# ScalarE's copies of the rotated keys: eight in a row, or one by one from the rounded tile

## The chip, the core and the metric

The kernel runs on one core of a Trainium2 chip. The metric is the device time of one execution in microseconds (us). Five engines work side by side, each through its own list of instructions in a fixed order: TensorE (PE in the profile; its weight loads are shown as PEld), VectorE (DVE), ScalarE (ACT), GpSimd (POOL) and SyncE (SP), which here issues nearly all the DMA transfers. An instruction that waits for a result of another engine holds up all that stands behind it in its own list.

## The reference

Two layers of a transformer trunk work on one sequence of 512 tokens with 1024 channels, in float32. Each layer does this:

```
h = rmsnorm(x);  proj = h @ w_in            # 6 x 512 columns: sb q,k,v and df q,k,v
sb_out = stick_breaking_attention(...)      # 8 heads of 64
dq, dk = rope(df_q), rope(df_k)             # 4 heads x 2 maps of 64
p = softmax(mask(dq . dk / 8))              # per head and map
df_out = rmsnorm((p[0] - lam * p[1]) @ df_v)
x = x + concat(sb_out, df_out) @ w_o
x = x + relu(rmsnorm(x) @ w_ff1)**2 @ w_ff2 # 4096 hidden channels
```

At the end comes one more rmsnorm. The change is in the keys `dk` of the differential attention, after the rotation by `rope`.

## The kernel before, in words

**Precision.** A float32 product is made of three matmuls. Each operand is split into a rounded high part (`hi`, made by a ScalarE copy) and the rest (`lo`, a VectorE subtraction); the function `three` (lines 258 to 260) multiplies hi by hi, lo by hi and hi by lo. The weights are split in the kernel too. They arrive as 512-KB units (`raw`, three buffers, issued by SP), and `split_part` makes `whi` on ScalarE (line 118) and `wlo` on VectorE (line 119), with two buffers of each. So `whi` of a unit waits until TensorE has done with the unit before the last.

**Order.** A layer begins with the projections in the order of the tuple `ORDER`: d0, w0, d1, d2, w1, d3, s0, u0 and so on. A `d` is one head of the differential group (q and k, 24 matmuls each), a `w` is its values, an `s` a pair of stick-breaking heads, a `u` their values. The generator `dense` gives these out in steps, and between the steps the generator `attn` gives out pieces of the attention of heads that are ready. A modelled clock (`clock[0]`, in us) decides how they are mixed, and `defer` hands a function over once that clock has gone on by a given time. The order in which the instructions are handed over is a priority; a scheduler at build time then lays down the list of each engine by its own estimate of durations. So a few instructions handed over later can change the lists of all engines.

**A `d` head.** `evict_d` (line 466 and after) multiplies the q and the k block in PSUM with `cos_t` and `sin_t` on VectorE (lines 469 and 470; tiles u and v). For k it defers `rest` by 3.5 us (`DLY_R`). There POOL subtracts and adds (lines 477 and 478), which gives two tiles: `u1` (named u0d1q and so on in the profile) with the first halves of all rotated vectors, and `v1` (v0d1q) with the second halves. Each tile holds q in partitions 0 to 63 and k in 64 to 127. Each is split into hi and lo (lines 205 and 206; h0d1k and l0d1k in the profile), and then the 32-row pieces are brought into the layout that the score matmuls want, once for each tile j and map m: four DMAs (line 446), two into the q stack (st..q, of hi and lo) and two into the stack of the keys' low parts (kl..), and two ScalarE copies of 32x512 into the stack of the keys' high parts (st..k, lines 493 and 494). That makes 16 DMAs and 8 copies for a head. The copies read the float32 tile (u1 or v1) and round it on the way, so they need POOL's result alone and not the split. The scores of the head may begin 10 us (`DLY_D`) of the modelled clock after `rest`.

**Scores.** `scores` puts 128 queries against up to 512 keys into a PSUM bank S (two buffers; lines 505 and 506). VectorE masks and takes the maximum (lines 545 to 550), ScalarE does the exponentials (line 558), and these release the bank for the scores after next. The weights p are normalised by DVE and POOL (lines 564 to 567), transposed on TensorE (line 586, T), split again (zh, zl, fh, fl) and multiplied with the values (O). The hi and lo tiles of the heads and the diagonal tiles of the norms (dgh, dgl) share one pool of four buffers (`tr`).

Of the kernel before, what the change touches and what calls it, by code (L numbers as in the profile page):

```python
# [9 lines left out]
F32 = mybir.dt.float32  # L10
F32R = mybir.dt.float32r
BF16 = mybir.dt.bfloat16
AF = mybir.ActivationFunctionType
# [24 lines left out]
RA, RB = (21, 8), (26, 16)  # L38
MAN = ()
_CTX = {}  # L40
DLY_R, DLY_D, DLY_S = 3.5, 10.0, 6.0
TAIL, ATT, DENSE, CAP = 6.0, 54.0, 145.0, 0.1
SBQ, SBK, SBV, DFQ, DFK, DFV = (i * 512 for i in range(6))
# [96 lines left out]
def trunk(ctx, tc, xT, w, gains, lamv, cos, sin, out):  # L140
    nc = tc.nc
# [62 lines left out]
    def split(hi, lo, src):  # L204
        nc.scalar.activation(hi, src, AF.Copy)  # L205
        nc.vector.tensor_tensor(out=lo, in0=src, in1=hi.bitcast(F32), op=ALU.subtract)  # L206
# [142 lines left out]
    for l in range(L):  # L349
        with ExitStack() as actx:  # L350
# [18 lines left out]
            def tt(name):  # L369
                return a2.tile([P, S], F32, tag="t", name=name, bufs=4)  # L370

            def tr(name):
                return a2.tile([P, S], F32R, tag="hl", name=name, bufs=4)
# [57 lines left out]
            def defer(delay, fn):  # L431
                later.append((clock[0] + delay, fn))
                later.sort(key=lambda e: e[0])

            def stack_tiles(kind, b, which):
                nm = f"{l}{kind}{b}{which}"
                i = "ds".index(kind) * 4 + b
                assert i < 2 or scored[i - 2] == (2 if i < 6 else 4), (nm, scored)
                out = [a2.tile([P, 2, S], F32R, tag="st" + which, name="st" + nm)]
                if which == "k":  # L440
                    out.append(a2.tile([P, 2, S], F32R, tag="kl", name="kl" + nm))
                stacks[(kind, b, which)] = out
                return out

            def move(dst, src):
                nc.sync.dma_start(dst.bitcast(F32), src.bitcast(F32))

            def evict_s(pt, kind, b, which):
# [14 lines left out]
                if which == "k":  # L463
                    ready[(kind, b)] = clock[0] + DLY_S

            def evict_d(pt, kind, b, which):
                nm = f"{l}{kind}{b}{which}"
                u, v = tt("u" + nm), tt("v" + nm)
                nc.vector.tensor_mul(u, pt, cos_t)
                nc.vector.tensor_mul(v, pt, sin_t)  # L470
                if which == "q":
                    heads[("x", b)] = (u, v)
                    return
                u1, v1 = heads.pop(("x", b))

                def rest():
                    nc.gpsimd.tensor_sub(u1, u1, v)
                    nc.gpsimd.tensor_add(v1, v1, u)
                    q, = stack_tiles(kind, b, "q")
                    k, kl = stack_tiles(kind, b, "k")  # L480
                    for j, o in enumerate((u1, v1)):
                        hi, lo = tr(f"h{nm}{j}"), tr(f"l{nm}{j}")
                        split(hi, lo, o)
                        d0 = slice(32 * j, 32 * j + 32)
                        d1 = slice(64 + 32 * j, 64 + 32 * j + 32)
                        for m in range(2):
                            rq = slice(32 * m, 32 * m + 32)
                            rk = slice(64 + 32 * m, 64 + 32 * m + 32)
                            move(q[d0, m, :], hi[rq, :])
                            move(q[d1, m, :], lo[rq, :])  # L490
                            move(kl[d0, m, :], lo[rk, :])
                            move(kl[d1, m, :], lo[rk, :])
                            nc.scalar.activation(k[d0, m, :], o[rk, :], AF.Copy)
                            nc.scalar.activation(k[d1, m, :], o[rk, :], AF.Copy)
                    ready[(kind, b)] = clock[0] + DLY_D

                defer(DLY_R, rest)

            def scores(pt, st, m, i):
# [405 lines left out]
```

## Time and profile before

Three runs took 1244.31, 1244.63 and 1246.58 us (median 1244.63). The profiled execution took 1240.59 us; its span from the first to the last instruction is 1238.8 us.

| engine | busy us | share of the span | instructions |
|---|---|---|---|
| PE | 1197.8 | 97% | 5978 |
| DVE | 685.4 | 55% | 1009 |
| ACT | 553.2 | 45% | 948 |
| POOL | 207.2 | 17% | 267 |

TensorE's granted clock over the span was 0.991. The projections and attention of layer 0 lie at about 5 to 270 us, those of layer 1 at about 615 to 880 us; the rest is the MLP. The shares are averages of very unlike stages: in the MLP ScalarE is busy for two to four tenths of the time, and in the stretches with the `d` heads for five to seven tenths. A row of a timeline gives the start, the duration, the engine, the line, the operation with output and inputs, and in brackets how long the engine was idle before and what ended that.

### The profile page before, as it was taken

What the parts mean: (1) busy time and instruction counts of PE and PEld (TensorE: products, weight loads), DVE (VectorE), ACT (ScalarE), POOL (GpSimd) and SP (SyncE); (2) the same over time, 40 slices, a digit from 0 to 9 for tenths busy, and PEclk for the clock granted to TensorE, in tenths of its full rate; (3) what the DMA queues carried; (4) which work ended last, traced back from release to release, by engine and by line L of the source; (5) the groups of instructions that cost most, each with busy time, mean ns of one, the idle gap of its engine ahead of it and who ended that gap; (6) DMA issues with size and microseconds to landing.
All of it is one profiled execution on the core that took longest, in us unless ns stands there. A gap on an engine that the chain in (4) does not pass through costs nothing. (4 is left out here: it accounts for less than half of the span.)

```text
span 1238.8 us, 15970 instructions
## 1 busy us (share of the span) xinstructions
PE 1197.8 (97%) x5978; PEld 1007.3 (81%) x5978; DVE 685.4 (55%) x1009; ACT 553.2 (45%) x948; POOL 207.2 (17%) x267
## 2 busy tenths in 40 slices
PE   7899999999999999999999999999999999999996
PEld 5787898888888888888887888888888888888886
DVE  6676779875443234433346867787644223444325
ACT  5665656654332224433346656665444212433214
POOL 4123354330000000001112225432200000000002
PEclk9999999999999999999999999999999999999998
DMA  6343435223322332332333354342333332322231
GB/s 209 104 122 113 132 98 151 86 71 102 102 90 98 102 97 90 102 101 88 100 97 115 96 143 113 100 128 64 101 95 94 102 99 89 101 102 86 93 94 68
DMA packets 46892, 128.20 MB, mean 103 GB/s; under 512 B 7264, under 2 KB 10336, under 8 KB 46816
## 3 DMA queue, kind: packets, MB, share of 16 engines
q1 hardware_dynamic: 46672, 127.17, 33.8%
q8 instruction: 47, 0.77, 0.2%
q14 instruction: 29, 0.24, 0.1%
q10 hardware_dynamic: 144, 0.02, 0.0%
HBM read 104.09 MB, written 2.10 MB: 86 GB/s over the span
## 5 line engine op out<-in xcount | busy, mean ns | idle before, releaser
L118 ACT ACTIVATE whi<-raw 128x1024 fp32r<-128x1024 f32 (+2 forms) x200 | 204.9, 1026 | 490.3 <-PE f L259 427.7
L119 DVE TENSOR_TENSOR wlo<-raw,whi 128x1024 fp32r<-128x1024 f32 (+2 forms) x200 | 247.6, 1239 | 164.2 <-ACT whi L118 162.8
L258 PE MATMUL f<-h_hi,whi 128*128 128x512 f32 x512 | 199.4, 389 | 0.0
L259 PE MATMUL f<-h_lo,whi 128*128 128x512 f32 x512 | 199.2, 389 | 0.0
L260 PE MATMUL f<-h_hi,wlo 128*128 128x512 f32 x512 | 199.2, 389 | 0.0
L259 PE MATMUL f<-ul,whi 128*128 128x512 f32 x496 | 193.0, 389 | 0.0
L258 PE MATMUL f<-uh,whi 128*128 128x512 f32 x496 | 193.0, 389 | 0.0
L260 PE MATMUL f<-uh,wlo 128*128 128x512 f32 x496 | 193.0, 389 | 0.0
L805 DVE SCALAR_TENSOR_TENSOR ft<-f,rbc 128x512 f32<-128x512 f32 x64 | 44.2, 691 | 164.0 <-PE f L260 163.1
L258 PEld LDWEIGHTS f<-h_hi,whi 128*128 128x128 f32 x512 | 96.1, 188 | 20.1
L260 PEld LDWEIGHTS f<-h_hi,wlo 128*128 128x128 f32 x512 | 96.1, 188 | 19.8
L259 PEld LDWEIGHTS f<-h_lo,whi 128*128 128x128 f32 x512 | 96.1, 188 | 19.8
L258 PEld LDWEIGHTS f<-uh,whi 128*128 128x128 f32 x496 | 93.1, 188 | 19.5
L260 PEld LDWEIGHTS f<-uh,wlo 128*128 128x128 f32 x496 | 93.1, 188 | 19.3
L259 PEld LDWEIGHTS f<-ul,whi 128*128 128x128 f32 x496 | 93.1, 188 | 19.2
L223 POOL TENSOR_TENSOR ssq<-ssq,sq 128x512 f32<-128x512 f32 x28 | 41.8, 1491 | 377.4 <-ACT sq L222 368.0
L834 DVE TENSOR_TENSOR x<-x,f 128x512 f32<-128x512 f32 x32 | 22.0, 687 | 103.1 <-PE f L260 103.1
L340 POOL TENSOR_TENSOR ssq<-ssq,sqf 128x256 f32<-128x256 f32 x6 | 4.4, 736 | 338.3 <-ACT sqf L338 335.0
L206 DVE TENSOR_TENSOR ul<-fu,uh 128x512 fp32r<-128x512 f32 x64 | 44.1, 692 | 0.4 <-ACT uh L205 0.4
L205 ACT ACTIVATE uh<-fu 128x512 fp32r<-128x512 f32 x64 | 40.5, 633 | 2.0
L806 ACT ACTIVATE fu<-ft 128x512 f32<-128x512 f32 x64 | 39.6, 618 | 1.6 <-DVE ft L805 1.6
L526 POOL TENSOR_TENSOR sig1s<-sig1s,C1s 128x128 f32<-128x128 f32 (+3 forms) x32 | 29.0, 907 | 53.0 <-DVE C1s L523 38.7
(650 smaller groups left out, 2301.2 us busy)
## 6 DMA issues: line engine op xcount, KB each, us to landing
raw<-in_w SPq DMA_DIRECT2D x176, 512.0 KB, 3.6
raw<-in_w SPq DMA_DIRECT2D x16, 448.0 KB, 3.2
x<-in_xT SPq DMA_DIRECT2D x8, 256.0 KB, 4.5
out_xT<-y SPq DMA_DIRECT2D x8, 256.0 KB, 2.4
raw<-in_w SPq DMA_DIRECT2D x8, 128.0 KB, 4.5
cos_t<-in_cos SPq DMA_DIRECT2D x2, 256.0 KB, 4.0
sin_t<-in_sin SPq DMA_DIRECT2D x2, 256.0 KB, 4.3
kl0d0k<-l0d0k SPq DMA_DIRECT2D x8, 64.0 KB, 2.0
```

The source lines that it names most:

```text
L118: nc.scalar.activation(hi[:, a:b], raw[:, a:b], AF.Copy)
L119: nc.vector.tensor_tensor(out=lo[:, a:b], in0=raw[:, a:b], in1=hi[:, a:b].bitcast(F32), op=ALU.subtract)
L205: nc.scalar.activation(hi, src, AF.Copy)
L206: nc.vector.tensor_tensor(out=lo, in0=src, in1=hi.bitcast(F32), op=ALU.subtract)
L223: eng.tensor_tensor(out=ssq, in0=ssq, in1=sq, op=ALU.add)
L258: nc.tensor.matmul(pt, ah, bh, start=first, stop=False)
L259: nc.tensor.matmul(pt, ah, bl, start=False, stop=False)
L260: nc.tensor.matmul(pt, al, bh, start=False, stop=last)
L526: nc.gpsimd.tensor_mul(sig[:, 0:wd], sig[:, 0:wd], C[:, 1 : wd + 1])
L805: nc.vector.scalar_tensor_tensor(out=t, in0=pt, scalar=0.0, in1=rbc, op0=ALU.max, op1=ALU.mult)
L806: nc.scalar.activation(uu, t, AF.Square)
L834: nc.vector.tensor_add(x[:, db, :], x[:, db, :], pt)
```

## The change

The two copies of each (j, m) are no longer handed over at once with the rest of the head. Each is handed to `defer` by itself: the first 0.9 us (`KC_GAP`) of the modelled clock after `rest`, the second 1.8 us, and so on to the eighth at 7.2 us. And a copy now reads the rounded tile `hi` (h0d1k in the profile) and not the float32 tile `o` (u0d1q or v0d1q). The copied values are the same, since a rounded value does not change when it is rounded again. The number and the shape of the instructions stay as they were.

```diff
+KC_GAP = 0.9
...
+            def copy_k(dst, src):
+                return lambda: nc.scalar.activation(dst, src.bitcast(F32), AF.Copy)
...
-                            nc.scalar.activation(k[d0, m, :], o[rk, :], AF.Copy)
-                            nc.scalar.activation(k[d1, m, :], o[rk, :], AF.Copy)
+                            for i, d_ in enumerate((d0, d1)):
+                                defer(KC_GAP * (4 * j + 2 * m + i + 1), copy_k(k[d_, m, :], hi[rk, :]))
```

## The prediction, made before the result was known

> **What bounds the kernel.** I read the page first:
>
> ```profile
> span 1238.8 us, 15970 instructions
> PE 1197.8 (97%) x5978; PEld 1007.3 (81%) x5978; DVE 685.4 (55%) x1009; ACT 553.2 (45%) x948; POOL 207.2 (17%) x267
> ```
>
> TensorE bounds the whole. A change on ScalarE can only add to or take from TensorE's idle 41 us, and from the time it works at a lower clock. So the second view is what TensorE waited for (total, times, longest):
>
> ```profile
> PE S0d L505 <- ACT p0d L558: 3.9, 3, 2.7
> PE S1d L505 <- ACT p1d L558: 3.6, 2, 2.0
> PE S1d L505 <- DMA st1d3q<-l1d3k: 2.7, 1, 2.7
> ...
> PE p1d1q L258 <- ACT whi L118: 2.1, 1, 2.1
> ...
> PE T0d L586 <- DVE fl0d L206: 1.6, 1, 1.6
> PE p0u L412 <- ACT whi L118: 1.5, 1, 1.5
> ```
>
> The first and second rows, the two with `whi`, and the DMA row (its source is a split of ScalarE's) stand behind ScalarE's list, where the copies are. Third, that list in time, ahead of the 2.1-us wait:
>
> ```profile
> 635.66 0.63 ACT L493 ACTIVATE st1d0k<-v1d0q 32x512 fp32r<-32x512 f32 x1 [5.26 <-POOL v1d0q L478]
> 636.31 0.63 ACT L494 ACTIVATE st1d0k<-v1d0q 32x512 fp32r<-32x512 f32 x1
> 636.96 0.63 ACT L205 ACTIVATE h1d0k<-u1d0q 128x512 fp32r<-128x512 f32 x1
> ...
> 641.49 0.63 ACT L494 ACTIVATE st1d0k<-v1d0q 32x512 fp32r<-32x512 f32 x1
> 642.14 1.06 ACT L118 ACTIVATE whi<-raw 128x1024 fp32r<-128x1024 f32 x1
> ```
>
> All eight copies and both splits of the head stand ahead of the weight split that TensorE needs at 641.1. Ahead of the 1.5-us wait it is the same:
>
> ```profile
> 111.69 0.63 ACT L205 ACTIVATE h0d3k<-u0d3q 128x512 fp32r<-128x512 f32 x1 [2.03 <-POOL u0d3q L477]
> ...
> 115.55 0.63 ACT L494 ACTIVATE st0d3k<-v0d3q 32x512 fp32r<-32x512 f32 x1
> 116.20 1.06 ACT L118 ACTIVATE whi<-raw 128x1024 fp32r<-128x1024 f32 x1
> ```
>
> Last, the clock by 1-us windows (length, PE, PEld, DVE, ACT and POOL busy, granted clock, DMA):
>
> ```profile
> 643.00:644.00 1.00, 0.73 (x2) 0.30 (x2) 0.78 (x1) 1.00 (x4) 0.00 (x0) 1.00 0.31 78
> 644.00:645.00 1.00, 0.50 (x1) 0.50 (x2) 1.00 (x3) 0.99 (x2) 0.00 (x0) 0.51 0.49 123
> 645.00:646.00 1.00, 1.00 (x4) 0.71 (x4) 1.00 (x2) 0.74 (x2) 0.00 (x0) 0.50 0.37 94
> ```
>
> After a long wait the clock is halved for some 3.4 us (here 644.0 to 647.4), which costs 1.7 us of TensorE's time. In the stages with attention this comes four times: after waits of 2.66 us (to 81.3), 1.50 and 0.87 us together (to 118.6), 2.14 us (to 643.3) and 2.68 us (to 728.9). It does not come after 1.90 us (33.6) or 2.05 us (685.2). So I charge 1.7 us for a wait above about 2.4 us.
>
> [...]
>
> **What the change moves.** No instruction is added. The 64 copies stay at 0.628 us (lines 493 and 494), 40.2 us of ScalarE. Sixteen of them now wait for a split on their own engine. The dependent pair fu, uh in the MLP has 0.04 us between them (302.94 + 0.61 to 303.59) against 0.01 between independent copies; the largest gap that the trace puts down to ScalarE itself is 0.38 us (before `whi` at 45.68). That is 0.5 to 6 us in all; I take 0.5, as the pair has the same shape, and it lies beside TensorE's work. The lists that the changed kernel's build lays down show the rest: `whi`, the splits and the exponentials move ahead of copies; no copy runs before the split of its tile; POOL does u0d3q before the 512-wide p0d, and the norm's small power before u1d3q; SP sends both hi pieces of a head first at heads 1 and 3 of layer 0 and one weight load earlier at head 3. I went through the waits one by one, with durations from rows.
>
> *Layer 1, head 0 (2.14 + 0.52 us, and clock).* ScalarE's list becomes h, copy, h, `whi`. POOL's u1d0q ends at 636.9, so `whi` runs from 638.9 to 640.0 and `wlo` to 641.3, in time for TensorE at 641.1 (`wlo` is needed at 641.6). Gain 2.66 + 1.7 = 4.4. Late next: the values' evictions (vdh, vdl) now stand behind six copies, and the bank for p1d1k comes free at 647.4 against 646.8: −0.6. The scores' DMAs, 16 issues of 0.6 us, end as before and stay just ahead.
>
> *Layer 0, head 3 (1.50 + 0.87 us, and clock).* u0d3q comes from POOL at 109.65 and not 111.66, as the 512-wide p0d (2.10 us there) follows it. Then h, four copies, `whi` from 112.9, `wlo` to 115.2; TensorE comes at 115.8. Gain 2.37 + 1.7 = 4.1. Late next: the second split's DMAs. DVE's l0d3k stays behind the next `wlo` and ends at 120.2; issue and landing take 2.2 us, while TensorE now comes at 122.7: 0 to 1.0 lost, I take 0.4. The wait of 1.59 at 146.06 (fl0d) goes, as the d3 chain before it is some 4 us earlier: +1.6 (0 to 1.6).
>
> *Head 0's exponentials.* Layer 0 (0.98 at 56.23, 0.24 at 62.50): they now precede head 1's copies and start at 53.8 instead of 55.4. +1.2, at the least +0.7. Layer 1 (1.53 at 662.86): they hang on POOL's u1d1q and p1d, not on copies: 0. The 1.12 us for `wlo` at 673.57 go, since `whi` moves up past copies: +1.1 (0 to 1.1).
>
> *Head 1's exponentials (2.66 at 81.31, 2.05 at 685.19).* This is where it costs. Two copies of v used ScalarE's idle time before u's split (69.75 to 71.02, 75.58 to 76.85). Now they come after it, and two stand ahead of the exponentials: 1.3 us later. Layer 0 starts 1.4 us earlier, so the wait is about 2.9 instead of 2.66, with the clock halved as before: −0.2. In layer 1 it grows from 2.05 to 2.95 and crosses the point where the clock falls: −0.9 − 1.7 = −2.6.
>
> *Layer 1, head 3 (2.68 at 728.91, and clock).* h of u runs 714.0 to 714.7 instead of 716.2 to 716.9, and l1d3k's second part, now ahead of a `wlo`, ends at 723.2 to 724.7 instead of 726.4. Its DMA lands up to 2.2 us later, by 725.5 to 727, against TensorE at 725.8. The wait is 0 to 1.2 and the clock stays: +1.5 + 1.7 = 3.2.
>
> The other waits (33.57, 40.55, 749.18, 751.06, the stick-breaking part, start and end) keep their causes: 0. Sum: 4.4 − 0.6 + 4.1 − 0.4 + 1.6 + 1.2 + 1.1 − 0.2 − 2.6 + 3.2 = 11.8, less 0.2 for the waits on own results in the critical lists: 11.6 us. Of these the least supported are the clock at head 3 and the 1.6 us at 146; halving 3.2 and 1.6 gives 9.2, and I take 9.0. The profiled execution (1240.59, span 1238.8 and 1.8 around it) would become 1231.6. It lies 4.0 under the median of the runs shown, so for the runs: **1235.6 us**.
>
> **Rivals.** *Slower: the exponentials everywhere end up behind copies.* What happens at head 1 would happen at the first scores of heads 1, 2 and 3 in both layers: six places, each 1.3 us of copies and 1.7 us of clock, 18 us, against the 11.6 with the 2.8 already charged at head 1 put back: 3.6 us slower, 1248. It decides from about five of six places on. For it: the two waits that exist. Against: at heads 2 and 3 TensorE did not wait at all before, and the lists put only two copies, or none, ahead of their first exponentials. 0.13.
>
> *No change: the gain is taken back at once.* From the end of p1d2k the chain DVE, POOL, split, copies, exponentials takes 11.6 us and does not get shorter; if the same holds at every head, a TensorE that is earlier only waits longer, and of the two large gains (7.5 us after what follows them) and the others about 1 us is left: 1243.6. For it: the 650 to 690 stretch, where DVE and ScalarE are busy two thirds of the time. Against: the wait at 118 has no such chain behind it. 0.10.
>
> *More than forecast.* No fall of the clock at 685 and the wait at 728 gone: 11.6 + 1.7 + 1.2, 14.5 us, 1230. 0.12, inside faster.
>
> *The copies stay where they are* is excluded: ScalarE's list is another.
>
> **How the numbers follow.** The likeliest case, 6 to 13 us faster (1231.6 to 1238.6), has 0.52; more than that 0.12; a smaller gain between 2.5 and 6 us 0.13; no change 0.10; slower 0.13. A change of 0.2% (2.5 us) is about what a measurement of this kernel can tell from none. So faster 0.77, same 0.10, slower 0.13. The range leaves out the upper part of slower and the far end of the gains: 1229.5 to 1245.5.
>
> **What would show it.** Right: no `whi` wait of TensorE at p1d1q and p0u, full clock around 120, 645 and 730, waits for p0d and p1d at head 1 of about 3 us. Wrong: `whi` still ending those waits (then it waits for a buffer and not for the list), waits for exponentials at heads 2 and 3, a new wait for DMAs at S0d of head 3 above 1 us, or idle time of TensorE that is not smaller than 41 us.

## The result, and the profile after

Changed kernel: 1238.54 us median (five executions, 1235.74 to 1238.88), against 1244.5 for the kernel before (five, 1242.51 to 1246.58). The ratio is 0.9945, 95% interval 0.9927 to 0.9962: faster by about 0.55%, where 9 us (0.7%) were forecast and 1235.6 us. The traced executions differ by less, 1238.78 against 1240.59, and for the trace 1231.6 was forecast. The page of the changed kernel, its first lines:

```profile
span 1237.0 us, 15976 instructions
PE 1198.4 (97%) x5978; PEld 1010.2 (82%) x5978; DVE 685.9 (55%) x1009; ACT 553.5 (45%) x948; POOL 212.4 (17%) x267
```

What TensorE waited for, the view that answers to the one of before:

```profile
PE S1d L509 <- ACT p1d L562: 5.4, 2, 4.3
PE S0d L509 <- ACT p0d L562: 4.6, 1, 4.6
PE S0d L509 <- ACT mdh L206: 2.9, 1, 2.9
PE S1d L509 <- ACT h1s0k L206: 2.5, 1, 2.5
...
PE T0d L590 <- DVE ms L231: 0.4, 1, 0.4
```

Both `whi` rows are gone, and so are the 1.6 us for fl0d. But the exponentials p0d and p1d cost up to 4.6 us at a time instead of 2.7, and two waits of 2.9 and 2.5 us stand at head 3. All of TensorE's waits together fell only from 34.0 to 31.7 us. Two things, then, have to be explained: where the gain at the weight splits went, and why the waits grew at heads 1 and 3.

ScalarE's list ahead of p1d1q, in time, with the split that TensorE needs:

```profile
637.91 0.63 ACT L206 ACTIVATE h1d0k<-u1d0q 128x512 fp32r<-128x512 f32 x1 [6.50 <-POOL u1d0q L481]
638.58 0.63 ACT L468 ACTIVATE st1d0k<-h1d0k 32x512 fp32r<-32x512 f32 x1
639.23 0.63 ACT L206 ACTIVATE h1d0k<-v1d0q 128x512 fp32r<-128x512 f32 x1
639.77 1.04 ACT L119 ACTIVATE whi<-raw 128x1024 fp32r<-128x1024 f32 x1
```

That is the list forecast: one copy ahead of `whi` instead of eight. TensorE takes `whi` at 641.94 without a wait. From the start of p1d0k to the start of p1d1k it was 27.9 us before (623.3 to 651.3) and is 23.9 now (624.3 to 648.2).

### The profile page after: what moved, and what is told of

It reads as the page before. It is cut to its first block, busy times and chain, and to the rows that moved or that the text cites. A ratio compares the mean times of both kernels' runs of the same rounds, so it can differ in the third digit from the quotient of the medians.

```text
span 1237.0 us, 15976 instructions
## 1 busy us (share of the span) xinstructions
PE 1198.4 (97%) x5978; PEld 1010.2 (82%) x5978; DVE 685.9 (55%) x1009; ACT 553.5 (45%) x948; POOL 212.4 (17%) x267
## 5 line engine op out<-in xcount | busy, mean ns | idle before, releaser
L530 POOL TENSOR_TENSOR sig1s<-sig1s,C1s 128x128 f32<-128x128 f32 (+3 forms) x32 | 32.0, 1001 | 49.6 <-DVE C1s L527 35.0
```

The source lines that it names most:

```text
L530: nc.gpsimd.tensor_mul(sig[:, 0:wd], sig[:, 0:wd], C[:, 1 : wd + 1])
```

## The experiments

Ratios are to the kernel before, in executions on the same chip, with 95% intervals. e1 to e4 ran beside each other on one chip, e5 to e7 later on the same chip, e8, e9 and e10 on another, e11 and e12 on a third. A ratio of one group is compared with one of another only through the kernel before, which ran in each.

### Which head costs: head 2 left as it was (e1), head 2 alone (e2)

In e1 the deferral and the rounded source stay at heads 0, 1 and 3, and head 2 gets the old form; e2 has the condition turned round (`b == 2`).

```diff
+                                if b != 2:
                                     defer(KC_GAP * (4 * j + 2 * m + i + 1), copy_k(k[d_, m, :], hi[rk, :]))
+                                else:
+                                    nc.scalar.activation(k[d_, m, :], o[rk, :], AF.Copy)
```

> Heads 0, 1 and 3 of both layers as in the changed kernel, head 2 as before (its eight copies issued at once, from the unsplit tile). Theory A (the copies of head 2 stand between its first split and the exponentials of head 1): two of head 2's copies fall back into ScalarE's idle time ahead of the split, so the exponentials of head 1 come 1.3 us earlier in each layer. TensorE's waits for p0d and p1d at S0d and S1d go from 4.59 and 4.35 us to about 3.3 and 3.05, the half clock behind each from 6.8 to 3.4 us, and the rest stays: 2 x (1.3 + 1.7) = 6.0 us less than the changed kernel, about 1232.5. Theory B (TensorE is only earlier, and the chain from the end of p0d2k through VectorE and GpSimd sets the exponentials, whatever ScalarE's list): the waits stay at 4.3 to 4.6 us and the time at 1237.5 to 1239.5.

> The counterpart: only head 2 of both layers has its copies handed over one by one from the split tile, the other heads are as before. Theory A: the gains at heads 0 and 3 are missing (the waits for whi at p1d1q and p0u stay at 2.1 and 1.5 us) and the loss is there: the waits at head 1 go from 2.66 and 2.05 us to about 3.9 and 3.3, with 1.7 us of half clock more in layer 1 and 0 or 1.7 in layer 0: 4 to 6 us slower than before, about 1249. Theory B: the waits at head 1 stay within 0.3 us of before and the time within 1 us of before, 1244.5.

Measured: e1 0.9948 (0.9931 to 0.9964), median 1235.2, its traced execution 1233.31. e2 0.9997 (0.9982 to 1.0012). In e1 the waits are 3.38 and 2.97 us, as theory A had them, with 3.4 us of half clock each. The time did not follow: 6 us less than the changed kernel were forecast, and the ratio is not to be told from the changed kernel's (0.9945 above, 0.9964 in e5 on this chip). What head 2 costs in time shows only in e7 against e6, below. ScalarE's list between the split of head 2 and the exponentials of head 1, layer 0, of the changed kernel:

```profile
76.94 1.06 ACT L119 ACTIVATE whi<-raw 128x1024 fp32r<-128x1024 f32 x1
78.02 1.27 ACT L468 ACTIVATE st0d2k<-h0d2k 32x512 fp32r<-32x512 f32 x2
79.29 0.37 ACT L562 ACTIVATE p0d<-S0d,sm0d 128x128 f32<-128x128 f32 x1
```

and of e1, where these two copies run in idle time ahead of the split:

```profile
68.11 1.27 ACT L501 ACTIVATE st0d2k<-v0d2q 32x512 fp32r<-32x512 f32 x2 [1.49 <-POOL v0d2q L482]
...
76.03 1.06 ACT L119 ACTIVATE whi<-raw 128x1024 fp32r<-128x1024 f32 x1
76.99 0.35 ACT L565 ACTIVATE p0d<-S0d,sm0d 128x128 f32<-128x128 f32 x1
```

From the start of the last matmul of p1d2k to the score matmul that waits, layer 1 takes 13.4 us before (671.8 to 685.19), 14.6 in the changed kernel, 14.8 in e2 and 13.3 in e1: two copies of 0.63 us, wherever head 2 is deferred. That much of theory A holds. It is not all of the longer wait (2.05 to 4.35): TensorE also arrives earlier, 10.3 us after that matmul instead of 11.3, since the wait of 1.12 us for `wlo` at 673.57 went. Theory B has this part.

e2 missed theory A's forecast of 1249; the time is theory B's, but the waits are not, which moved by 0.6 and 1.15 us. In layer 0 the copies of before do not only stand ahead of the exponentials; they stand ahead of `whi`, so VectorE's `wlo` and the reductions behind it come late too. Deferred copies let `whi` pass, and the wait fell there from 2.66 to 2.06, while it rose in layer 1 to 3.20. The same edit helps one layer and hurts the other.

### The two halves of the change: deferral alone (e3), source alone (e4)

```diff
-                return lambda: nc.scalar.activation(dst, src.bitcast(F32), AF.Copy)
+                return lambda: nc.scalar.activation(dst, src, AF.Copy)
...
-                                defer(KC_GAP * (4 * j + 2 * m + i + 1), copy_k(k[d_, m, :], hi[rk, :]))
+                                defer(KC_GAP * (4 * j + 2 * m + i + 1), copy_k(k[d_, m, :], o[rk, :]))
```

and for e4

```diff
-                                defer(KC_GAP * (4 * j + 2 * m + i + 1), copy_k(k[d_, m, :], hi[rk, :]))
+                                copy_k(k[d_, m, :], hi[rk, :])()
```

> All heads deferred as in the changed kernel, but the copies read the unsplit tile (u1, v1), as before. Theory A: ScalarE's list at head 0 of layer 1 is that of the changed kernel up to whi (split, one copy, split, whi), and at head 3 of layer 0 four copies stand between the first split and whi, so both whi waits stay gone; two copies of head 2 go into idle time ahead of the split, so the waits at head 1 are 0.7 to 1.3 us shorter than in the changed kernel: 1233 to 1236. Rival C (it is the source, the split tile, that moves the copies): the waits for whi are back, 1243 to 1245.

> The copies read the split tile, but are all issued at once, without the deferral. Theory A: in layer 1, head 0, whi stands behind four copies and the second split instead of behind six copies, so 1.2 to 1.4 us of the 2.66 us stay as a wait and the clock stays whole (gain about 1.3 + 1.7); at head 3 of layer 0 the list is that of the changed kernel, the whi wait is gone and the DMA wait with its 6.8 us of half clock is there; at head 1 all eight copies follow the split, so the waits are 4.3 us and more as in the changed kernel: 1239 to 1242. Rival C: the source does all, 1238.5 as in the changed kernel. Rival D (without the deferral the source changes nothing): 1244.5.

Measured: e3 0.9966 (0.9953 to 0.9979), e4 0.9968 (0.9948 to 0.9988). Either half gives about what the whole gives, and the two do not add. The times forecast under theory A were missed on both sides (1237.7 where 1233 to 1236 was put, 1237.9 where 1239 to 1242 was). In e4 0.7 us of `whi` are left at p1d1q where 1.2 to 1.4 were expected. In e3 the waits at head 1 are 2.92 and 4.07 us; the first is less than in the changed kernel, by more than expected, the second by 0.3 only. Rivals C and D fall, C by the waits and not by the time of e4, which is what C gave: each half moves the list by itself.

### What TensorE meets at head 3, and the clock: the changed kernel again (e5), a load put back (e6), both (e7), a second load (e10)

e6 adds to the changed kernel, and e7 to e1, an order on SP's queue: the load of weight tile 18 stays behind the last lo piece of head 3. e10 adds tile 113 to e7.

```diff
+HOLD = (18,)
...
+                if i in HOLD:
+                    self.tc.add_manual_dep(ld.ins, self.last.ins.name,
+                        mybir.DependencyInfo(mybir.DependencyClass.NoSync, mybir.DependencyReason.DATA), reason="hold")
```

> The changed kernel once more, beside the two that follow. Theory W (the traces so far: half-clock stretches of TensorE begin and end on a grid of 3.41 us that has a fixed phase within one execution and another phase in the next, .93 of a period in the changed kernel's, .68 in that of before): the waits at head 1 and head 3 come out again within 0.3 us of 4.59, 2.85, 4.35 and 2.45, while the stretches of half clock begin at another phase and each may be 0, 3.4 or 6.8 us long; executions spread over 3 to 5 us with the granted clock from 0.985 to 0.991. Theory L (a wait above about 2.4 us always halves the clock for 3.4 us, a longer one for 6.8): the stretches are the same as in the first trace, 6.8 us each at head 1 of both layers and at head 3 of layer 0 and none at 728.

> The changed kernel, with the 512-KB load of weight tile 18 kept behind the last lo piece of head 3 on SP in layer 0 (as it stood before the change); nothing else moves. Theory D (TensorE's 2.85 us at S0d of head 3 are the landing time of those pieces behind two 512-KB loads, 4.9 us against 2.4 with one): the first lo piece is issued at the same time, lands 2.4 to 2.6 us later, the wait falls to 0.3 to 0.9 us and the half clock behind it goes: 2.0 to 2.5 us, and 1.7 or 3.4 more where the first trace had 6.8 us of half clock, 3.5 to 6 in all: about 1234. Theory S (VectorE's l0d3k and SP's issue times set it, not the landing): the wait stays above 2.4 us and the time at 1238.

> Both at once: head 2's copies as before (as in e1) and the load of weight tile 18 behind head 3's pieces (as in e6). If the two are independent, the gains add: waits of about 3.4 and 3.0 us at head 1, 0.3 to 0.9 at head 3 of layer 0, 2.7 left at head 3 of layer 1; 4 to 6 us less than e1's profiled 1233.3, so 1228 to 1231 for a trace of the same clock, and 6 to 10 us less than the changed kernel. If the gain of one is taken back by the other (TensorE earlier, the chain unchanged): 1233 or more.

> e7 with the load of weight tile 113 kept behind the last lo piece of head 3 in layer 1 too. If the landing behind one 512-KB load costs 1.0 to 1.4 us there (3.4 against 2.0 to 2.4 us in the traces), the wait of 2.77 us at S1d of head 3 falls to 1.4 to 1.8 and the time by 1 to 3 us against e7. Rival: tile 113 is then late itself, its load lands 4 us later, and TensorE waits for whi or wlo at p1u instead: no gain, or up to 3 us more.

Measured: e5 0.9964 (0.9951 to 0.9976), e6 0.9960 (0.9948 to 0.9973), e7 0.9924 (0.9912 to 0.9937), e10 0.9905 (0.9890 to 0.9920; median 1230.97, the lowest here, but not to be told from e8's 0.9916 on the same chip).

*The landing.* SP's queue in the changed kernel, start and duration; the first row holds two issues, at 119.07 and 121.33:

```profile
119.07 2.59 SPq L107 DMA_DIRECT2D raw<-in_w  x2
121.93 0.51 SPq L447 DMA_DIRECT2D st0d3q<-l0d3k  x1
```

In e6 there is one such load, at 119.97, and the piece is issued at 122.82, when VectorE has just made it.

The DMA view of that one piece (size, us from issue to landing) in the changed kernel:

```profile
st0d3q<-l0d3k SPq DMA_DIRECT2D x1, 64.0 KB, 4.9
```

Issued at 121.93, it lands at 126.85, and S0d starts at 126.94: the row "ACT mdh" among the waits is this DMA. With one 512-KB load ahead the same piece takes 2.4 us (before), 2.3 (e6) and 2.6 (e9); with two, the later one issued only 0.6 us ahead of the piece, 4.9, 5.5 (e5), 4.8 (e1), 6.1 (e8) and 5.0 (e11). Theory D holds for the cause. It was too high for the gain: TensorE's list puts S0d earlier in e6, so the wait only fell from 3.40 (e5) to 1.71 us, and e6's time is not to be told from e5's. With head 2 as before as well, e7 is 3.9 us faster than e6 (1233.28 against 1237.18, and no execution of the one is as slow as the fastest of the other): head 2's deferral, from the other side. That is 4.4 us less than e5, where 6 to 10 were forecast if the gains added, and its wait at head 3 is 1.28 us. e10's wait at S1d fell from 2.77 to 1.86, a little above the 1.4 to 1.8 forecast, and tile 113 was not late; its ratio is 0.0019 (2.4 us) below e7's, but the two intervals overlap.

*The clock.* e5 is the same program as the changed kernel. Its waits came out at 4.54, 3.40, 4.38 and 3.05 us; the two at head 3 are 0.55 and 0.60 longer than in the first trace, by a longer landing, and outside the 0.3 of theory W. What differs more is the half clock. The busy time by windows of 3.41 us at the waits of head 3 (length, then PE, PEld, DVE, ACT and POOL, granted clock, DMA). First trace of the changed kernel, two windows in layer 0 and the one of the wait in layer 1:

```profile
122.62:126.04 3.42, 1.47 (x11) 1.16 (x9) 1.93 (x3) 2.82 (x5) 1.27 (x1) 1.00 0.77 220
126.04:129.45 3.41, 2.51 (x12) 2.54 (x13) 1.97 (x3) 0.25 (x1) 0.00 (x0) 0.50 0.69 167
...
726.78:730.20 3.42, 1.66 (x14) 1.69 (x15) 2.24 (x3) 1.81 (x4) 1.51 (x1) 1.00 0.58 181
```

and e5, two in layer 0 and two in layer 1:

```profile
122.22:125.64 3.42, 1.63 (x12) 1.32 (x10) 1.77 (x3) 2.84 (x6) 1.27 (x1) 1.00 0.67 208
125.64:129.05 3.41, 1.80 (x15) 1.83 (x16) 2.12 (x3) 0.41 (x1) 0.00 (x0) 1.00 0.65 159
722.96:726.38 3.42, 0.37 (x4) 0.36 (x4) 2.29 (x3) 2.57 (x5) 0.77 (x1) 1.00 0.70 228
726.38:729.79 3.41, 3.41 (x19) 3.41 (x18) 0.69 (x1) 0.63 (x1) 0.72 (x1) 0.50 0.69 166
```

A wait of 2.85 us cost 6.8 us of half clock in one execution, and one of 3.40 us at the same place cost none in the next, where it lay across the edge of two windows (busy 1.63 and 1.80). Theory L falls.

### Head by head: head 0 (e8), head 3 (e9), heads 0 and 3 (e11), heads 0 and 1 (e12)

The diff is that of e1, with `b == 0`, `b == 3`, `b in (0, 3)` and `b < 2`.

> Only head 0 of both layers has its copies handed over one by one from the split tile; heads 1 to 3 as before. Theory G (the change's gain is head 0's alone, that of head 3 is taken by the landing of its pieces, head 2's deferral loses): no wait for whi at p1d1q, p1d1k starts 3 to 4 us earlier than in before against p1d0k; the wait for whi at p0u stays at 1.5 us and the one at S1d of head 3 at 2.7; the waits at head 1 near 3.4 and 3.0 us: 3.5 to 5.5 us less than before, a ratio of 0.9957 to 0.9972. Theory P (the steps as they were predicted, head 0 and head 3 about half of the gain each): 4.4 - 0.6 + 1.2 + 1.1 = 6.1 us less, 0.9951, with head 3's 7 us to come from the next run.

> Only head 3 of both layers. Theory G: the waits at p0u (1.50 and 0.87 us) go, and TensorE meets a wait of 2.3 to 3.4 us at S0d of head 3 in their place, while the one at S1d of head 3 stays at 2.2 to 3.1: within 1.5 us of before, a ratio of 0.9988 to 1.0012. Theory P: 4.1 - 0.4 + 3.2, with the 1.6 at 146, 7 to 8.5 us less than before, 0.9932 to 0.9944.

> Heads 0 and 3 of both layers with copies handed over one by one from the split tile, heads 1 and 2 as before. Theory A+ (the gains of head 0 and head 3 alone add: 0.9916 and 0.9976, so the loss in the whole change is that of heads 1 and 2): 13 us less than before, a ratio of 0.988 to 0.9905. Theory T (they do not add: a TensorE that head 0 has made earlier meets the landing of head 3's pieces, 2.1 to 2.9 us at S0d and S1d of head 3, and the clock that goes with it): 7 to 10 us less, 0.992 to 0.9945, no faster than head 0 alone.

> Heads 0 and 1, heads 2 and 3 as before. Theory A+: if the loss sits with head 1 (its copies now stand between the exponentials of head 0 and the split of head 2), the waits at S0d and S1d of head 1 are 3.0 to 3.5 us as in e1 and not 2.5 and 1.75 as in e8, with 3.4 us of half clock each: 3 to 6 us slower than head 0 alone, a ratio of 0.994 to 0.9965. Theory T: head 1 changes nothing by itself, 0.991 to 0.993.

Measured: e8 0.9916 (0.9904 to 0.9928; median 1231.97), e9 0.9976 (0.9964 to 0.9989), e11 0.9937 (0.9923 to 0.9952), e12 0.9919 (0.9903 to 0.9934). Head 0 alone is worth 10 us, more than any theory gave it and more than the whole change: its interval lies below e5's. Head 3 alone is worth 3 us, so theory G, which gave it nothing, is wrong there, and so is theory P, which gave it 7 to 8.5. In e9 TensorE meets no wait at S0d of head 3, but 0.28 us for `whi` and 0.88 for `wlo` stay at p0u, and 3.07 at S1d. The two heads do not add: e11 is 0.2% slower than e8, as theory T had it, though this is barely clear of the noise.

Head 1 does not change the time (e12), but it does change the waits. TensorE at head 1 in e12:

```profile
PE S1d L512 <- ACT p1d L565: 4.1, 2, 3.0
PE S0d L512 <- ACT p0d L565: 3.4, 1, 3.4
```

They are those of e1, 3.38 and 2.98 us, as theory A+ had them, against 2.50 and 1.75 in e8. In return smaller waits ahead of them are gone: 0.85 and 0.50 us in layer 0 (at 55.6 and 66.7 in e8), 0.38 and 0.32 in layer 1 (at 665.8 and 667.1). From head 0's scores to head 1's the waits add up to 3.9 us in e8 and 3.4 in e12 in layer 0, and to 3.5 and 4.1 in layer 1. TensorE waits at another place for about as long.

TensorE's waits in e11 at head 3:

```profile
PE S0d L512 <- ACT mdh L206: 3.0, 1, 3.0
...
PE S1d L512 <- ACT rb L254: 2.7, 1, 2.7
```

and in e8, at head 3 and at the weights ahead of it:

```profile
PE S0d L512 <- DMA st0d3q<-l0d3k: 2.1, 1, 2.1
...
PE S1d L512 <- DMA st1d3q<-l1d3k: 0.9, 1, 0.9
...
PE p0u L420 <- DVE wlo L120: 0.9, 1, 0.9
PE p1u L420 <- DVE wlo L120: 0.9, 1, 0.9
...
PE p1u L413 <- ACT whi L119: 0.5, 1, 0.5
```

In layer 0, e8 waits 0.88 and then 2.08 us at head 3, e11 2.97 in one piece: the same sum. In layer 1 it is 0.49, 0.88 and 0.94 (2.3 us) against 2.72. Behind a head 0 that is deferred already, moving head 3's copies does not shorten the chain that ends in the landing of its pieces; only the place where TensorE waits for it changes. In pieces the waits cost no clock, in one piece 3.4 us of half clock each. The waits at head 1 are the same in both, 2.50 and 1.75. Between 60 and 760 us, e8 has 3.4 us of half clock, the kernel before 13.7 (four windows), the changed kernel 20.5 and e5 17.1.

## Why the prediction was right, and where its steps failed

The direction is right and 1238.5 lies in the range. The sum of 11.6 us does not stand: two groups of steps held, the others were paid back or did not come, and the price of the clock did not hold as a rule. Between the traces, the sum had layer 0 gain 6.3 us and layer 1 5.5. The changed kernel is 1.0 us behind at the end of layer 0's attention (274.1 against 273.1) and gains 2.8 after it; e5 is 1.4 ahead and gains 1.5. That the medians differ by 6.0 us and come within 3 us of the forecast is so in part by luck: the execution traced before lay 4 us under its median and that of the changed kernel at its own. The prediction's own signs came out mixed. The waits for `whi` went, but the waits at head 1 are not about 3 us, and the new wait at S0d of head 3, which it named as a sign of being wrong, is there.

- **Layer 1, head 0** (4.4 − 0.6 = 3.8): right. 4.1 us measured from p1d0k to p1d1k, with a wait of 0.4 for the bank where 0.6 was put; no half clock at 644. e8 has the same 4.1 us.
- **Head 0's exponentials, layer 0** (1.2) and **the wait for fl0d at 146** (1.6): right. Both waits are gone, p0d2k starts 1.5 us earlier against p0d1q, and 0.4 us are left of the 1.6 (for `ms`, at 158). It is head 1's deferral that removes the first wait: 0.85 of its 0.98 us are left in e8 and none in e12.
- **The wait for `wlo` at 673.57** (1.1): it went and gained nothing. TensorE came 1.1 us earlier to the exponentials of head 1 and waited there. This is the rival "taken back at once", at this place.
- **Head 1's exponentials** (−0.2 and −2.6): the mechanism was right, two copies of head 2 behind its split, 1.3 us in layer 1. The waits forecast, 2.9 and 2.95, came out at 4.59 and 4.35. In layer 0 the exponentials come only 0.2 us later against p0d2k (15.0 us after the start of its last matmul instead of 14.8), but TensorE is there 10.4 us after it instead of 12.1: its list has eight matmuls of p0w and four of T0d fewer ahead of that score, which I had not looked at. In both layers the wait then cost 6.8 us of half clock and not 3.4. From p0d2k to p0d3q 2.7 us were lost, from p1d2k to p1d3q 3.0.
- **Layer 0, head 3** (4.1 − 0.4): the waits for `whi` and `wlo` went as forecast. The term that failed is "issue and landing take 2.2 us": they took 4.9, behind the second 512-KB load, which the change had moved ahead of the pieces. I had seen that load move and costed it at nothing. It does not move by head 3's own copies: two loads stand ahead in e8 (head 0 alone) and one in e9 (head 3 alone). The 2.37 us came back as 2.85. From the start of the last matmul of p0s0k to the start of p0s1q it was 21.8 us before, 22.6 in the first trace of the changed kernel (6.8 us of it at half clock), 20.5 in e5 (none) and 19.3 in e9, where one load stood ahead: the step pays 2.5 us where it meets no late landing. (Ahead of the wait at 117 only one split of the head stood before `whi`, not both as at 641.)
- **Layer 1, head 3** (3.2): the first split ran at 715.6 and not at 714.0, since POOL finished u1d3q only then. VectorE's second split ended at 725.2, half a microsecond behind the forecast's upper end, and the landing took 3.2 us (725.21 to 728.46) behind a load issued 0.9 us earlier, so the wait stayed at 2.45 (3.05 in e5). The 2.1 us by which the stretch from p1s0k to p1s1q is shorter in the first trace are the clock, which did not fall there; in e5 it fell and nothing was gained.
- **The clock** ("half clock after waits above 2.4 us"): wrong as a rule, and the fall at 644.0, after a wait of 2.14 us, did not fit it from the start. In the traces it goes by windows of 3.41 us and the work that is left in them, below, where I had reasoned with lengths of waits: a window with 1.42 us of work (123.5 in e11) was followed by half clock, and the wait of 2.05 us before left 1.55 in its window (681.6) and was not.

Of the rivals, "slower" charged six places and none but the two known ones came. "No change" named the right mechanism and its place (650 to 690). Head 0 alone gave 10 us in the medians and 8.6 between the traces, and not the 6.1 of its steps. The traces show where. e8 leads the kernel before by 0.6 us at 25 us, ahead of the first copy, by 2.4 at the end of layer 0's attention (271 us), by 6.5 at p1d1k and by 8.7 at 751 us. So layer 1's head 0 gives the 4.1 us. In layer 0, head 1's exponentials let the score start 13.6 us after p0d2k's last matmul starts instead of 14.8, although the code of heads 1 and 2 is that of before: ScalarE's list was laid down anew there, with the second split of head 2 at 74.0 and not 76.5 us. At 729 the half clock is gone, 1.7 us. By kind, 5.0 of the 8.6 us are waits (34.0 to 29.0) and 3.6 TensorE's shorter busy time (1197.8 to 1194.2). How much of this another build or another phase of the clock would give stays open.

## What to carry to other kernels

Handing ScalarE's copies over later moved the lists of the other engines too: POOL's u0d3q went ahead of p0d, and one weight load on SP ahead of head 3's pieces. After each wait that goes, look for the next thing that TensorE needs on that chain, here a landing behind weight loads or a reduction, and count only what is shorter up to there. An edit that pays at one place of a loop can be put at that place alone: the copies deferred at head 0 only beat the change at all heads.

## What the runs showed of the hardware that was not expected

*Half clock in windows of 3.41 us.* What follows is read off the granted clock in the views of this case's 14 traces (the kernel before, the changed kernel, e1 to e12). In each of them all starts and ends of half clock between 60 and 760 us lie on one grid of 3.413 us (in the changed kernel's first trace 78.27, 126.05 and 682.43: 14 and 177 periods apart), and the grid's phase differs from one execution to the next (0.68 of a period in the trace of before, 0.93 and 0.80 in the two of the changed kernel). TensorE's work in a window is taken here as its busy time by the clock it had. Between 60 and 760 us every window under 1.43 us (44 of them) was followed by one at half clock, of 18 between 1.44 and 1.67 four were, and none with 1.7 or more. A window that was busy throughout at half clock has 1.71 and was followed by full clock. Between 1.44 and 1.67 busy time does not settle it: 1.55 us were followed by full clock in the trace of before (681.6), 1.66 us by half clock in e11 (676.5). The count is of this stretch of these traces alone.

There, a stretch of idle time that left 1.7 us of work in its window cost nothing more, a longer one cost 1.7 us or not by where it fell, and waits of 2.85 and 4.35 us held the clock down for two windows (from 126.05 and 682.43 in the changed kernel). Ahead of 60 us, the wait of 1.90 us for v0d0q (to 33.6 in the trace of before, and as long in the changed kernel, e8 and e11) was followed by half clock in e11 (from 34.8) and in e12 (from 33.2), and not in the trace of before or in the first of the changed kernel. The spread between executions goes with the clock: for the kernel before, 15 executions at a mean clock of 0.990 took 1241.7 us on average, 12 at 0.987 took 1243.9.

*A large load just ahead on the queue.* On SP's queue the 64-KB piece of head 3 told of above (the first lo piece of its second half) took in layer 0 2.3 to 2.6 us to land behind one 512-KB load that was issued 1.6 to 2.9 us earlier (the kernel before, e6, e9), and 4.8 to 6.1 behind two of which the later was issued 0.6 us earlier (the changed kernel, e1, e5, e8, e11). In layer 1 it took 2.5 us behind one issued 1.6 us earlier (the kernel before) and 3.2 behind one issued 0.9 us earlier (the changed kernel). A single load can stand for as much when it is near: the first lo piece of head 3's first half took 3.9 us in the changed kernel, behind one load issued 0.6 us earlier (113.44, the piece at 114.03), and 1.9 in the kernel before, with the last load 3.7 us ahead (109.59 and 113.30). One case does not fit, and no run shows why: in e3 the piece took 4.4 us behind one load issued 1.6 us earlier. In the six cases of which the views give both landings, the piece landed 0.2 to 0.4 us after the load ahead of it (126.85 and 126.68 in the changed kernel; the others are its two single loads, both layers of the kernel before, and e9). So the later the load landed, the later the piece did.
